# A gated-delta decode step: state products in two column halves, state updates in two row groups

## The chip, the core and the metric

The kernel runs on one core of one Trainium2 chip. The metric is device time in microseconds (us), the median over several executions. A profiled execution gives the trace.

## What is computed

One inference step of a one-layer hybrid decoder. A prompt of 2048 tokens and a group of 8 samples with 4 new tokens each go through the same weights: an adaptive layer norm, a wide input projection, a gated MLP branch and a gated DeltaNet branch with 8 heads, output projections and a last layer norm. All of it is in f32. The change lies in the DeltaNet branch, where each sample brings an old state per head:

```python
def step(S, xs):
    q_n, k_n, u_n, w_n, qk_n, gc_n = xs
    v_new = u_n - jnp.einsum('bhck,bhkv->bhcv', w_n, S)
    o = (jnp.einsum('bhck,bhkv->bhcv', q_n * jnp.exp(gc_n)[..., None], S)
         + jnp.einsum('bhcs,bhsv->bhcv', qk_n, v_new))
    g_last = gc_n[..., -1:]
    S = (S * jnp.exp(g_last)[..., None]
         + jnp.einsum('bhck,bhcv->bhkv', k_n * jnp.exp(g_last - gc_n)[..., None], v_new))
    return S, o
```

For the sample group this is one step for 8 samples of 4 tokens. A state `S` is 128x128, one for each sample and head.

## The kernel before

The prompt is worked in two halves of 1024 tokens; the 32 sample tokens ride along with the first half as 32 more columns. `main` (L953) walks a list of projections: for each weight column block of 128, every column group of the half (384, 384 and 256+32 tokens in the first half, 512 and 512 in the second) is a chain of 24 matmuls into one PSUM bank, operands split in a high and a low part (`project`, L906). These matmuls are the bulk of the kernel. In each half the first part of the list goes head by head: k, q, v and z of head h, then some gate columns. Beside it each head has its own streams: the token-major copies, the gram products, the inverse of a unit triangular matrix (`inverse`, L1412) and the recurrence over 8 chunks (`chain`, L1523). In the first half each head also has `sample_head` (L1631), the sample's recurrence, so it runs eight times.

All of these streams are Python generators. They yield an operation with an estimated duration, and the planner (`Sched.run`, L135) picks at each step the stream whose operation could start first by its model: each engine has a time at which it is free, and an operation may start `LAG` after what it depends on (L41: 400 ns for PE, 200 for ACT, DVE and POOL). Priorities break ties. The order in which the planner takes the operations is the order in which they are written to the engines' queues, and each engine works its queue in that order. Buffers are handed out by name (`_acquire`, L74). PSUM's 8 banks are `mm` (banks 0 to 2, projections), `po` (3 and 4, outputs of the chain) and `pt` (5 to 7, all else); `pu` is any of 3 to 7 (L294 to L297). `kx` is one buffer; `Rb` and `Xb` are two each, shared with the chain.

Operations are written by small helpers, so their trace lines are the helpers': L438 a matmul, L443 a transpose, L395 an ACT operation, L404, L414 and L420 DVE operations. Where a block yields once and then writes several matmuls itself, the line is its own: L641 (conditioning, four column quarters), L1470, L1476, L1479 (32x32 products of the inverse), L1496, L1507, L1509 (64x64 products).

In `sample_head` the steps that matter are these. k, q and v are made token-major (32 partitions), `kp` and `vs` are scaled rows of k and v, and `us` is the 32x32 inverse. `kx` holds, per sample, 64 columns: 32 for k and 32 for decayed q, nonzero only in that sample's four. Eight products (L1693 to L1695), one for each sample, 64 columns against the sample's 128x128 state, add up in one accumulation of 64 partitions: S^T k in partitions 0 to 31, S^T q in 32 to 63. DVE forms `vs` minus the first (L1698), ACT takes the second out (L1702). The product with `us` (L1705) gives the new v. It goes into the output product (L1709) and, after the states have been scaled by their decay (L1729), into the updates: twice, for four samples each, DVE spreads the new v over four column blocks with the selection constants `c_sel` (L1733), one product of 32 rows, 128 columns and 512 moving columns makes four updates (L1736), and DVE adds them to the states (L1739).

An f32 product is two records in the trace: two passes, each with its own weight load.

Of the kernel before, what the change touches and what calls it, by code (L numbers as in the profile page):

```python
# [11 lines left out]
ALU = mybir.AluOpType  # L12

P = 128
# [3 lines left out]
NB = 8  # L18
LS = 4
NS = NB * LS  # L20
# [149 lines left out]
def hybrid_step_kernel(ctx: ExitStack, tc: tile.TileContext, x_prompt, x_sample, state_conv, state_ssm,  # L170
# [4 lines left out]
    nc = tc.nc  # L175
# [39 lines left out]
    def V(off, *dims, p0=0, np_=P):  # L215
        dims = [[1, d] if isinstance(d, int) else list(d) for d in dims]
        t, o, st = place(off)
        return bass.AP(t.tensor, t.offset + p0 * st + o, [[st, np_]] + dims)

    def Q(bank, off, *dims, p0=0, np_=P):  # L220
        dims = [[1, d] if isinstance(d, int) else list(d) for d in dims]
        return bass.AP(PS.tensor, PS.offset + p0 * 4096 + bank * 512 + off, [[4096, np_]] + dims)
# [93 lines left out]
    S = Sched(98 + len(unit_names), roles)  # L316
# [13 lines left out]
    c_mns, c_sts, c_trb, c_sel = const(32), const(32), const(32), const(8)  # L330
# [3 lines left out]
    c_sbeta, c_sneg, c_sngc, c_kds = const(8), const(8), const(8), const(8)  # L334
# [46 lines left out]
    def act(out, in_, func=AF.Copy, dep=None, scale=None, bias=None, accum=None):  # L381
        ns = fsz(out) / 1.2 + (55 if in_ps(in_) else 95)
        ns += 93 * (not isinstance(scale, (int, float, type(None)))) + 93 * (bias is not None) + 150 * (accum is not None)
        if func in (AF.Ln, AF.Exp, AF.Tanh, AF.Gelu_apprx_tanh):
            ns += 1300 * ((func == AF.Ln) != S.ln_table)
            S.ln_table = func == AF.Ln
        t = yield ("o", "ACT", ns, dep)
        kw = {}
        if scale is not None:
            kw["scale"] = scale  # L390
        if bias is not None:
            kw["bias"] = bias
        if accum is not None:
            kw["accum_out"] = accum
        nc.scalar.activation(out, in_, func, **kw)  # L395
        return t
# [4 lines left out]
    def tt(out, a, b, op, dep=None, eng="DVE"):  # L401
        if eng == "DVE":
            t = yield ("o", "DVE", dve_ns(out, (a, b)), dep)
            nc.vector.tensor_tensor(out=out, in0=a, in1=b, op=op)  # L404
        else:
            t = yield ("o", "POOL", 240 + 2.15 * fsz(out), dep)
            nc.gpsimd.tensor_tensor(out=out, in0=a, in1=b, op=op)  # L407
        return t

    def ts(out, a, s1, op0, s2=None, op1=None, dep=None):  # L410
        aps = sum(not isinstance(s, (int, float, type(None))) for s in (s1, s2))
        t = yield ("o", "DVE", dve_ns(out, (a,), 1.0 if in_ps(a) else 2.0) + 60 * aps, dep)
        kw = dict(op1=op1) if op1 is not None else {}
        nc.vector.tensor_scalar(out=out, in0=a, scalar1=s1, scalar2=s2, op0=op0, **kw)  # L414
        return t

    def stt(out, a, s, b, op0, op1, dep=None):
        aps = not isinstance(s, (int, float))
        t = yield ("o", "DVE", dve_ns(out, (a, b)) + 60 * aps, dep)
        nc.vector.scalar_tensor_tensor(out=out, in0=a, scalar=s, in1=b, op0=op0, op1=op1)  # L420
        return t
# [14 lines left out]
    def mm(out, lhsT, rhs, start=True, stop=True, dep=None):  # L436
        t = yield ("o", "PE", pe_ns(lhsT, rhs), dep)
        nc.tensor.matmul(out, lhsT, rhs, start=start, stop=stop)  # L438
        return t
# [6 lines left out]
    def bc(ap, shape):  # L446
        return ap.to_broadcast(shape)
# [65 lines left out]
    def init_small():  # L513
        yield ("o", "DMA", 200.0, 0.0)
        nc.sync.dma_start(out=V(c_ong, 1), in_=DV(onorm_g, 0, [1, P], [1, 1]))
        nc.sync.dma_start(out=V(c_negA, 8), in_=DV(a_log, 0, [0, P], [1, 8]))
        nc.sync.dma_start(out=V(c_dtb, 8), in_=DV(dt_bias, 0, [0, P], [1, 8]))
        t = S.dma
        t = yield from act(V(c_negA, 8), V(c_negA, 8), AF.Exp, dep=t)
        t = yield from ts(V(c_negA, 8), V(c_negA, 8), -1.0, ALU.mult)  # L520
        t = yield from ts(V(c_ong, 1), V(c_ong, 1), 0.5, ALU.mult)
        S.signal("small", t)

    def init_vec():
        yield ("w", ("ada", 0))
# [1105 lines left out]
    def sample_head(h):  # L1631
        me = hd(0, h)
        t = 0.0
        for s in range(3):
# [24 lines left out]
        t = yield from ts(V(o_vf, 1, **k32), V(o_n, 1, **k32), 0.25, ALU.mult)  # L1659
        t = yield from pow_(V(o_vf, 1, **k32), V(o_vf, 1, **k32), 1)  # L1660
        kp, vs = x + 64, x + 192
        t = yield from ts(V(kp, P, **k32), Q(pb[0], 0, P, **k32), V(o_kf, 1, **k32), ALU.mult)
        t = yield from ts(V(vs, P, **k32), Q(pb[0], P, P, **k32), V(o_vf, 1, **k32), ALU.mult)
        S.release(pb, t)
        es, npq, am, m2, us = x + 320, x + 352, x + 416, x + 448, x + 480
        t1 = yield from tt(V(es, NS, **k32), V(gr, NS, **k32), V(c_mns, NS, **k32), ALU.add, dep=t1)
        t1 = yield from act(V(es, NS, **k32), V(es, NS, **k32), AF.Exp, bias=V(c_sngc + h, 1, **k32))
        egr = x + 32
# [4 lines left out]
                           bc(V(es, NS, **k32).unsqueeze(1), [NS, 2, NS]), ALU.mult, ALU.mult, dep=max(t, t1))  # L1673
        t = yield from tt(V(npq, NS, **k32), V(npq, NS, **k32), V(c_sts, NS, **k32), ALU.mult)
        t = yield from tp(Q(pb[0], 64, NS, **k32), V(npq, NS, **k32))
        t = yield from act(V(am, NS, **k32), Q(pb[0], 64, NS, **k32))
        t = yield from mm(Q(pb[0], 96, NS, **k32), V(am, NS, **k32), V(npq, NS, **k32))
        t = yield from tt(V(m2, NS, **k32), Q(pb[0], 96, NS, **k32), V(c_ident, NS, **k32), ALU.add)
        t = yield from mm(Q(pb[0], 128, NS, **k32), V(am, NS, **k32), V(m2, NS, **k32))
        t = yield from tt(V(us, NS, **k32), V(m2, NS, **k32), Q(pb[0], 128, NS, **k32), ALU.subtract)  # L1680
        S.release(pb, t)

        kb = yield ("a", "kx")
# [4 lines left out]
        nc.gpsimd.tensor_copy(V(kx, [68, 8], [1, 4]), V(sm, [4, 8], [1, 4]))  # L1688
        t3 = yield from tt(V(kx + 32, [68, 8], [1, 4]), V(sm + 32, [4, 8], [1, 4]), V(egr, [4, 8], [1, 4]),
                           ALU.mult, dep=max(t3, t2))  # L1690
        pb = yield ("a", "pt")
        t4 = 0.0
        for b in range(NB):  # L1693
            t4 = yield from mm(Q(pb[0], 0, P, np_=64), V(kx + 64 * b, 64), V(sb0[0] + b * P, P),
                               start=b == 0, stop=b == NB - 1, dep=max(t3, td, pb[2]))  # L1695
        S.release(kb, t4)
        rb = yield ("a", "Rb")
        t = yield from stt(V(rb[0], P, **k32), Q(pb[0], 0, P, **k32), V(c_sneg + h, 1, **k32), V(vs, P, **k32),  # L1698
                           ALU.mult, ALU.add, dep=max(t4, t, rb[2]))
        osb = yield ("a", "Xb")  # L1700
        q32 = dict(p0=32, np_=32)
        t5 = yield from act(V(osb[0], P, **q32), Q(pb[0], 0, P, **q32), dep=max(t4, osb[2]))  # L1702
        S.release(pb, max(t, t5))
        pb = yield ("a", "pt")
        t = yield from mm(Q(pb[0], 0, P, **k32), V(us, NS, **k32), V(rb[0], P, **k32), dep=max(t, pb[2]))  # L1705
        t = yield from act(V(rb[0], P, **k32), Q(pb[0], 0, P, **k32))
        tx = t

        t = yield from mm(Q(pb[0], P, P, np_=64), V(npq, 64, **k32), V(rb[0], P, **k32), dep=t)  # L1709
# [8 lines left out]
        t = yield from tp(Q(pb[0], 0, NS), V(osb[0], P, **q32), idn=V(c_ident + 32, NS, **q32), dep=max(t, pb[2]))  # L1718
        S.release(osb, t)
        tz = yield ("w", ("zz", 0, h, len(CG[0]) - 1))  # L1720
        ys = x + 448
        t = yield from stt(V(ys, NS), Q(pb[0], 0, NS), V(c_ong, 1), V(me["ZZ"][0] + HALF, NS),
                           ALU.mult, ALU.mult, dep=max(t, tz))
        S.release(pb, t)
# [3 lines left out]

        t2 = yield from tt(V(sb0[0], [P, 8], [1, P]), V(sb0[0], [P, 8], [1, P]),  # L1729
                           bc(V(egr + 3, [4, 8]).unsqueeze(2), [P, 8, P]), ALU.mult, dep=max(t2, t4))  # L1730
        for i in range(2):
            xe = yield ("a", "kx")
            t1 = yield from tt(V(xe[0], [P, 4], [1, P], **k32), bc(V(rb[0], P, **k32).unsqueeze(1), [NS, 4, P]),  # L1733
                               bc(V(c_sel + 4 * i, 4, **k32).unsqueeze(2), [NS, 4, P]), ALU.mult, dep=max(tx, xe[2]))
            pb = yield ("a", "pt")
            t = yield from mm(Q(pb[0], 0, 512), V(kp, P, **k32), V(xe[0], 512, **k32), dep=max(t1, pb[2]))  # L1736
            S.release(xe, t)
            a = V(sb0[0] + 512 * i, 512)
            t = yield from tt(a, a, Q(pb[0], 0, 512), ALU.add, dep=max(t, t2))  # L1739
            S.release(pb, t)  # L1740
        S.release(rb, t1)
        S.release(xb, max(t, S.ev[("smpdone", h)]))
        S.release(ss, t)
# [483 lines left out]
    def start():  # L2227
        S.spawn(x_take(0), 0.0)
        for i, j in enumerate((2, 0, 3, 1)):
            S.spawn(ada_block(j), 1.02 + 0.01 * i)  # L2230
        for c in range(9):
            S.spawn(x_norm(0, c, "xh0"), 1.0 + 0.001 * c)
        for cgi in range(3):
            S.spawn(x_done(cgi), 1.0)
            for k in range(KT):
                S.spawn(h_part(cgi, k), 1.5 + 0.1 * cgi + 0.01 * k)
# [16 lines left out]
    with tc.manual_schedule():  # L2253
        S.spawn(init_consts(), 0.0)
        S.spawn(init_ada(), 0.0)
        S.spawn(init_vec(), 1.015)
        start()
        S.spawn(init_small(), 1.02)
        S.spawn(wstream(groups), 1.0)
        S.spawn(main(), 9.0)  # L2260
        S.spawn(scal_free(), 5.0)
        S.spawn(conv_tail(), 3.0)
        S.spawn(v_take(), 1.0)
        S.spawn(inv_next(), 1.0)
        S.run()
# [37 lines left out]
```

## Time and profile before

| | us |
|---|---|
| median of 3 runs | 2743.01 |
| lowest, highest | 2738.87, 2744.91 |
| the profiled execution, its own time | 2741.66 |
| span of its instructions | 2739.8 |

In the profile PE is TensorE's matmuls and PEld its weight loads, DVE is VectorE, ACT ScalarE, POOL GpSimd. Matmuls are pipelined, and a record reaches from its start to the (modelled) end of its way through the array, so neighbouring records overlap. A form such as `128*64 128x128` is rows*columns of the array, then partitions x elements that move. In the timeline, neighbours of one line, operation and tiles stand in one row with their count: the row's length reaches from the first one's start to the last one's end.

### The profile page before, as it was taken

The numbers are of one execution on the slowest core, as the hardware profiler recorded it, in microseconds if no ns is written. First come the engines' busy times: TensorE is split into PE (matmuls) and PEld (weight loads), VectorE is DVE, ScalarE is ACT, GpSimd is POOL, SyncE is SP. The second block draws the span as 40 slices with busy tenths as digits, with TensorE's granted clock in tenths as the row PEclk, the third lists the DMA queues.
The fourth block names the chain that finished last, engine by engine and source line by source line (L and its number), as shares of the span: only waits on it lengthen the run. The fifth ranks groups of instructions, "written<-read, shape, count | busy, mean of one in ns | idle before, by whom it ended". The sixth has DMA issues, their size and how long they took to land. (4 is left out here: it accounts for less than half of the span.)

```text
span 2739.8 us, 43826 instructions
## 1 busy us (share of the span) xinstructions
PE 2692.0 (98%) x16514; PEld 2362.1 (86%) x16514; DVE 1445.9 (53%) x3194; ACT 1003.2 (37%) x2710; POOL 553.5 (20%) x1452
## 2 busy tenths in 40 slices
PE   6999999999999999999999999999999999999998
PEld 4989989998898999999997888788888888888876
DVE  5677666767552253433547655666663324433446
ACT  5544444545343322221224535444452312222120
POOL 2053444335300000000000443433341000000001
PEclk9999999999999999999999999999999999999999
DMA  6222332222553142233433222222223422233342
GB/s 213 59 70 70 84 90 63 74 69 62 152 190 95 58 125 77 86 111 92 138 109 102 79 77 69 69 61 66 77 59 92 123 95 80 71 114 104 104 124 84
DMA packets 360493, 255.88 MB, mean 93 GB/s; under 512 B 72793, under 2 KB 326033, under 8 KB 360282
## 3 DMA queue, kind: packets, MB, share of 16 engines
q1 hardware_dynamic: 360282, 253.10, 31.3%
q8 instruction: 129, 2.11, 0.3%
q14 instruction: 82, 0.67, 0.1%
HBM read 197.31 MB, written 55.71 MB: 92 GB/s over the span
## 5 line engine op out<-in xcount | busy, mean ns | idle before, releaser
L438 PE MATMUL psum<-TX,TWHL 128*128 128x384 f32 (+3 forms) x9296 | 1981.7, 361 | 3.8 <-DVE TX L404 3.4
L438 PEld LDWEIGHTS psum<-TX,TWHL 128*128 128x128 f32 (+1 forms) x9296 | 1551.8, 188 | 165.1 <-issue 10.8
L395 ACT ACTIVATE arena<-psum 128x128 bf16<-128x128 f32 (+8 forms) x920 | 311.8, 348 | 777.7 <-PE psum L438 620.8
L427 POOL TENSOR_TENSOR arena<-arena 128x1 f32<-128x1 f32 (+4 forms) x139 | 125.4, 903 | 1627.7 <-DVE arena L414 1412.2
L420 DVE SCALAR_TENSOR_TENSOR arena<-arena 128x512 f32<-128x512 f32 (+8 forms) x625 | 344.9, 561 | 92.3 <-ACT arena L395 81.0
L407 POOL TENSOR_TENSOR arena<-arena 128x60 f32<-128x60 f32 (+24 forms) x992 | 343.3, 346 | 132.7 <-DMA arena<-d_blk 26.7
L404 DVE TENSOR_TENSOR TWHL<-arena,TWHL 128x512 fp32r<-128x512 f32 (+1 forms) x344 | 235.4, 689 | 244.0 <-ACT TWHL L395 241.7
L420 DVE SCALAR_TENSOR_TENSOR arena<-arena,psum 128x128 f32<-128x128 f32 (+3 forms) x342 | 132.4, 403 | 361.2 <-PE psum L438 249.8
L395 ACT ACTIVATE TWHL<-arena 128x512 fp32r<-128x512 f32 x344 | 214.8, 627 | 206.8 <-PE psum L438 100.7
L395 ACT ACTIVATE arena<-arena 128x128 f32<-128x128 f32 (+8 forms) x509 | 228.3, 486 | 130.6 <-DVE arena L420 81.3
L443 PE MATMUL psum<-arena 128*128 128x128 f32 (+6 forms) x509 | 126.0, 271 | 2.5 <-ACT Y3F L395 0.8
L404 DVE TENSOR_TENSOR arena<-arena 128x3 f32<-128x3 f32 (+13 forms) x259 | 113.7, 447 | 18.6 <-DMA arena<-d_gc 8.7
L438 PE MATMUL psum<-arena 128*128 128x128 f32 (+6 forms) x524 | 101.6, 293 | 1.0 <-ACT arena L395 1.0
L420 DVE SCALAR_TENSOR_TENSOR arena<-psum,arena 128x512 f32<-128x512 f32 (+4 forms) x80 | 39.9, 510 | 109.8 <-PE psum L438 109.6
L1219 POOL COPY arena<-arena 128x3 f32<-128x3 f32 x120 | 35.8, 298 | 296.8 <-ACT arena L395 296.1
L438 PEld LDWEIGHTS psum<-arena 128*128 128x128 f32 (+5 forms) x524 | 73.8, 163 | 22.4 <-issue 12.7
L443 PEld LDWEIGHTS psum<-arena 128*128 128x128 f32 (+6 forms) x509 | 67.5, 137 | 26.4 <-issue 13.3
L395 ACT ACTIVATE Y7F<-psum 32x256 f32<-32x256 f32 (+6 forms) x115 | 46.6, 406 | 100.2 <-PE psum L438 39.0
L395 ACT ACTIVATE TX<-arena 128x512 fp32r<-128x512 f32 (+2 forms) x84 | 47.1, 586 | 93.1 <-DMA arena<-d_yb 75.7
L395 ACT ACTIVATION_READ_ACCUMULATOR arena<-psum 128x1 f32 (+1 forms) x392 | 76.6, 195 | 0.0
L414 DVE TENSOR_SCALAR arena<-arena 128x3 f32<-128x3 f32 (+10 forms) x234 | 47.6, 211 | 36.0 <-ACT arena L395 24.9
L404 DVE TENSOR_TENSOR TX<-arena,TX 128x512 fp32r<-128x512 f32 (+2 forms) x84 | 52.2, 638 | 24.8 <-ACT TX L395 24.4
(242 smaller groups left out, 2715.2 us busy)
## 6 DMA issues: line engine op xcount, KB each, us to landing
arena<-in_w_in_dram SPq DMA_DIRECT2D x288, 256.0 KB
out_dram<-arena SPq DMA_DIRECT2D x25, 512.0 KB
arena<-in_x_prompt_dram SPq DMA_DIRECT2D x24, 512.0 KB
arena<-d_gc SPq DMA_DIRECT2D x16, 512.0 KB
arena<-d_blk SPq DMA_DIRECT2D x64, 128.0 KB
d_yb<-arena SPq DMA_DIRECT2D x32, 256.0 KB
d_vh<-arena SPq DMA_DIRECT2D x16, 512.0 KB
arena<-d_vh SPq DMA_DIRECT2D x16, 512.0 KB
```

The costliest lines, as they stand in the source:

```text
L395: nc.scalar.activation(out, in_, func, **kw)
L404: nc.vector.tensor_tensor(out=out, in0=a, in1=b, op=op)
L407: nc.gpsimd.tensor_tensor(out=out, in0=a, in1=b, op=op)
L414: nc.vector.tensor_scalar(out=out, in0=a, scalar1=s1, scalar2=s2, op0=op0, **kw)
L420: nc.vector.scalar_tensor_tensor(out=out, in0=a, scalar=s, in1=b, op0=op0, op1=op1)
L427: nc.gpsimd.tensor_tensor(out=out, in0=a, in1=e, op=ALU.pow)
L438: nc.tensor.matmul(out, lhsT, rhs, start=start, stop=stop)
L443: nc.tensor.transpose(out, in_, ident[: in_.shape[0], : in_.shape[0]] if idn is None else idn)
L1219: nc.gpsimd.tensor_copy(V(c_tail + gi, [24, 3]), V(x0 + n0, 3))
```

## The change

In `sample_head` the eight state products are written as one block of the planner. Samples 0, 2, 4 and 6 accumulate in partitions 0 to 63 of the bank, samples 1, 3, 5 and 7 in partitions 64 to 127, so that they use the two column halves of the array. ACT then copies the upper half to SBUF, DVE adds the lower half, and the subtraction reads that sum. The inverse `us` is written twice side by side, so that the product with it puts the new v into partitions 0 to 31 and 32 to 63; `kp` is copied to partitions 32 to 63 as well, and so are four columns of the selection constants, once, at the start. One DVE operation over 64 partitions then spreads the new v for all eight samples, and the two update products are written as one block, one from partitions 0 to 31 and one from 32 to 63 (two row groups of the array), into two banks, the second from `pu`. Some scratch columns move to make room.

```diff
+    def init_sel():
+        t = yield ("w", ("ada", 0))
+        yield from ts(V(c_sel, 4, p0=32, np_=32), V(c_sel + 4, 4, np_=NS), 1.0, ALU.mult, dep=t)
...
         t = yield from ts(V(kp, P, **k32), Q(pb[0], 0, P, **k32), V(o_kf, 1, **k32), ALU.mult)
+        t = yield from ts(V(kp, P, p0=32, np_=32), V(kp, P, **k32), 1.0, ALU.mult, dep=t)
...
-        es, npq, am, m2, us = x + 320, x + 352, x + 416, x + 448, x + 480
+        es, npq, am, m2, us = x + 320, x + 352, x, x + 320, x + 416
...
-        t = yield from act(V(am, NS, **k32), Q(pb[0], 64, NS, **k32))
+        t = yield from act(V(am, NS, **k32), Q(pb[0], 64, NS, **k32), dep=max(t, t2))
...
-        t = yield from tt(V(us, NS, **k32), V(m2, NS, **k32), Q(pb[0], 128, NS, **k32), ALU.subtract)
+        t = yield from tt(V(us, [NS, 2], [1, NS], **k32), bc(V(m2, NS, **k32).unsqueeze(1), [NS, 2, NS]),
+                          bc(Q(pb[0], 128, NS, **k32).unsqueeze(1), [NS, 2, NS]), ALU.subtract)
...
-        t4 = 0.0
+        t4 = yield ("o", "PE", 4 * 230.0, max(t3, td, pb[2]))
         for b in range(NB):
-            t4 = yield from mm(Q(pb[0], 0, P, np_=64), V(kx + 64 * b, 64), V(sb0[0] + b * P, P),
-                               start=b == 0, stop=b == NB - 1, dep=max(t3, td, pb[2]))
+            nc.tensor.matmul(Q(pb[0], 0, P, p0=64 * (b % 2), np_=64), V(kx + 64 * b, 64), V(sb0[0] + b * P, P),
+                             start=b < 2, stop=b >= NB - 2)
         S.release(kb, t4)
-        rb = yield ("a", "Rb")
-        t = yield from stt(V(rb[0], P, **k32), Q(pb[0], 0, P, **k32), V(c_sneg + h, 1, **k32), V(vs, P, **k32),
-                           ALU.mult, ALU.add, dep=max(t4, t, rb[2]))
         osb = yield ("a", "Xb")
         q32 = dict(p0=32, np_=32)
-        t5 = yield from act(V(osb[0], P, **q32), Q(pb[0], 0, P, **q32), dep=max(t4, osb[2]))
-        S.release(pb, max(t, t5))
+        o64 = V(osb[0], P, np_=64)
+        t4 = yield from act(o64, Q(pb[0], 0, P, p0=64, np_=64), dep=max(t4, osb[2]))
+        t4 = yield from tt(o64, Q(pb[0], 0, P, np_=64), o64, ALU.add)
+        S.release(pb, t4)
+        t5 = t4
+        rb = yield ("a", "Rb")
+        t = yield from stt(V(rb[0], P, **k32), V(osb[0], P, **k32), V(c_sneg + h, 1, **k32), V(vs, P, **k32),
+                           ALU.mult, ALU.add, dep=max(t4, t, rb[2]))
         pb = yield ("a", "pt")
-        t = yield from mm(Q(pb[0], 0, P, **k32), V(us, NS, **k32), V(rb[0], P, **k32), dep=max(t, pb[2]))
-        t = yield from act(V(rb[0], P, **k32), Q(pb[0], 0, P, **k32))
+        t = yield from mm(Q(pb[0], 0, P, np_=64), V(us, 64, **k32), V(rb[0], P, **k32), dep=max(t, pb[2]))
+        t = yield from act(V(rb[0], P, np_=64), Q(pb[0], 0, P, np_=64))
...
-        for i in range(2):
-            xe = yield ("a", "kx")
-            t1 = yield from tt(V(xe[0], [P, 4], [1, P], **k32), bc(V(rb[0], P, **k32).unsqueeze(1), [NS, 4, P]),
-                               bc(V(c_sel + 4 * i, 4, **k32).unsqueeze(2), [NS, 4, P]), ALU.mult, dep=max(tx, xe[2]))
-            pb = yield ("a", "pt")
-            t = yield from mm(Q(pb[0], 0, 512), V(kp, P, **k32), V(xe[0], 512, **k32), dep=max(t1, pb[2]))
-            S.release(xe, t)
+        xe = yield ("a", "kx")
+        t1 = yield from tt(V(xe[0], [P, 4], [1, P], np_=64), bc(V(rb[0], P, np_=64).unsqueeze(1), [64, 4, P]),
+                           bc(V(c_sel, 4, np_=64).unsqueeze(2), [64, 4, P]), ALU.mult, dep=max(tx, xe[2]))
+        pb = yield ("a", "pt")
+        pc = yield ("a", "pu")
+        t = yield ("o", "PE", 900.0, max(t1, pb[2], pc[2]))
+        for i, q in enumerate((pb, pc)):
+            rows = dict(p0=32 * i, np_=32)
+            nc.tensor.matmul(Q(q[0], 0, 512), V(kp, P, **rows), V(xe[0], 512, **rows), start=True, stop=True)
+        S.release(xe, t)
+        te = t
+        for i, q in enumerate((pb, pc)):
             a = V(sb0[0] + 512 * i, 512)
-            t = yield from tt(a, a, Q(pb[0], 0, 512), ALU.add, dep=max(t, t2))
-            S.release(pb, t)
+            t = yield from tt(a, a, Q(q[0], 0, 512), ALU.add, dep=max(te, t2))
+            S.release(q, t)
```

## Rows read from the trace of the kernel before

**Rows 1.** Page, parts 1, 2: busy us (share of span); granted clock.

```profile
PE 2692.0 (98%) x16514; PEld 2362.1 (86%) x16514; DVE 1445.9 (53%) x3194; ACT 1003.2 (37%) x2710; POOL 553.5 (20%) x1452
PEclk9999999999999999999999999999999999999999
```

**Rows 2.** Table of waits, PE, 170 to 745 us: total us, times, longest.

```profile
PE psum L438 <- ACT arena L395: 0.7, 1, 0.7
PE psum L1507 <- ACT Y7F L395: 0.7, 1, 0.7
```

**Rows 3.** Groups by form, PE: rows*columns, moving; busy us, mean ns.

```profile
L438 PE MATMUL psum<-arena 128*64 128x128 f32 x128 | 16.3, 277 | 0.0
L438 PE MATMUL psum<-arena 32*128 32x512 f32 x32 | 17.9, 640 | 0.0
L438 PE MATMUL psum<-TX,TWHL 128*128 128x288 f32 x1920 | 305.0, 303 | 0.0
L1496 PE MATMUL psum<-arena,Y3F 64*64 64x64 f32 x128 | 5.9, 236 | 0.0
```

**Rows 4.** Timeline, PE, head 3's state products: start us, length us.

```profile
389.14 1.96 PE L438 MATMUL psum<-arena 128*64 128x128 f32 x16
391.03 0.53 PE L438 MATMUL psum<-TX,TWHL 128*128 128x288 f32 x2
```

**Rows 5.** Timeline, PE: 64x64 column halves; four column quarters.

```profile
415.67 0.68 PE L1496 MATMUL psum<-arena,Y3F 64*64 64x64 f32 x16
33.32 1.06 PE L641 MATMUL psum<-Y4F,Y7F 128*32 128x512 f32 x8
```

**Rows 6.** Timeline, PE, around head 3's first update.

```profile
403.12 0.56 PE L438 MATMUL psum<-TX,TWHL 128*128 128x288 f32 x3
403.61 1.12 PE L438 MATMUL psum<-arena 32*128 32x512 f32 x2
404.66 0.53 PE L438 MATMUL psum<-TX,TWHL 128*128 128x288 f32 x2
```

**Rows 7.** Timeline, PE, head 0's state products in pieces.

```profile
180.58 1.09 PE L438 MATMUL psum<-arena 128*64 128x128 f32 x8
181.60 0.33 PE L443 MATMUL psum<-arena 128*128 128x128 f32 x1
...
183.28 0.44 PE L438 MATMUL psum<-TX,TWHL 128*128 128x384 f32 x1
```

**Rows 8.** Timeline, PE, 32x32 products of the inverse.

```profile
411.39 0.69 PE L1470 MATMUL psum<-arena,Y3F 32*32 32x32 f32 x32
```

**Rows 9.** Timeline, DVE, ACT, PE behind head 3's state products.

```profile
391.14 0.34 DVE L420 SCALAR_TENSOR_TENSOR arena<-psum,arena 32x128 f32<-32x128 f32 x1 [4.86 <-PE psum L438]
391.52 0.27 ACT L395 ACTIVATE arena<-psum 32x128 f32<-32x128 f32 x1 [0.27 <-DVE arena L420]
392.29 0.40 PE L438 MATMUL psum<-arena 32*32 32x128 f32 x2
...
393.78 0.43 PE L438 MATMUL psum<-arena 32*64 32x128 f32 x2
```

**Rows 10.** Groups by form, DVE, 160 to 760 us.

```profile
L404 DVE TENSOR_TENSOR arena<-arena 32x512 f32<-32x512 f32 x16 | 10.8, 675 | 0.0
L414 DVE TENSOR_SCALAR arena<-arena 32x128 f32<-32x128 f32 x8 | 2.5, 316 | 3.5 <-POOL arena L427 3.4
L404 DVE TENSOR_TENSOR arena<-psum,arena 32x128 f32<-32x128 f32 x8 | 2.3, 284 | 11.9 <-PE psum L438 11.8
```

**Rows 11.** Windows: length, busy us (PE, PEld, DVE, ACT, POOL), clock, DMA.

```profile
400.00:490.00 90.00, 90.00 (x663) 82.24 (x661) 61.94 (x156) 43.14 (x146) 34.39 (x93) 1.00 0.27 72
750.00:755.00 5.00, 5.00 (x54) 4.02 (x44) 0.71 (x2) 1.72 (x5) 0.00 (x0) 0.66 0.27 92
```

**Rows 12.** Timeline, head 0's last reads of Y0, head 2's first write.

```profile
226.98 0.61 PE L438 MATMUL psum<-arena,Y0F 128*128 128x128 f32 x4
230.40 0.55 DVE L420 SCALAR_TENSOR_TENSOR Y0F<-arena 128x384 f32<-128x384 f32 x1
```

More of the change, by code (lines that the diff above doesn't have):

```diff
@@ L1720, in sample_head @@
         tz = yield ("w", ("zz", 0, h, len(CG[0]) - 1))
-        ys = x + 448
+        ys = x + 320
         t = yield from stt(V(ys, NS), Q(pb[0], 0, NS), V(c_ong, 1), V(me["ZZ"][0] + HALF, NS),
@@ L2256, in hybrid_step_kernel @@
         S.spawn(init_vec(), 1.015)
+        S.spawn(init_sel(), 1.6)
         start()
```

## The prediction

> **What bounds the kernel now.** I read the page first. TensorE (PE) is busy for 2692.0 us, 98% of the span, with nine tenths or more of the full clock granted in all 40 slices; no other engine passes 53% [rows 1]. An average can hide stages, so I looked next at the one stage that the change touches: the eight heads of the first half, from about 170 to 745 us, in which the sample's recurrence is threaded between the big projections. There the table of waits names two idle spells of PE, 0.7 us each, in 575 us [rows 2]. PE is the bound of this stage, and it is fed: what is taken off its queue should come off the time nearly whole. Work on VectorE (DVE), ScalarE (ACT) and POOL counts only if PE comes to wait for it.
>
> The groups by form then give the two kinds of PE work that are changed [rows 3]. The products with the states (128 rows, 64 columns, 128 moving columns) are 128 passes: 8 heads x 8 products, and each f32 product is two passes. The updates (32 rows, 128 columns, 512 moving columns) are 32 passes: 8 heads x 2 products x 2 passes.
>
> **Cost of the products with the states.** In head 3 (a row's second number reaches to the end of its last pass) the 16 passes start at 389.14 and the next projection pass starts at 391.03: 1.89 us [rows 4]. The row is 1.96 long and a pass lasts 0.28 [rows 3], so the last starts 1.68 after the first: 15 steps of 0.112. The change sends even samples to partitions 0-63 and odd ones to 64-127 of the same bank, so two chains of four products could run side by side. What does a step of such a pair cost? The nearest rows are in the inverse and at the start. L1496 runs 64x64 products in alternating column halves: 16 passes in 0.68 [rows 5], of which the last is 0.24 [rows 3], so 0.44 for the steps before it. With 64 columns, half of 128, one after the other they would need 15 steps of about 0.056, or 0.84; as 8 pairs it is 7 steps of 0.063. L641 uses all 128 rows and four column quarters with 512 moving columns: 8 passes in 1.06 [rows 5], where one update's 2 passes with as many moving columns take 1.12 [rows 6]. So column tiles do overlap, also with all rows in use. For 128 moving columns I add the 0.056 that 64 more cost a step: 0.063 + 0.056 = 0.119 a pair, 7 steps, 0.83 in place of 1.68. Saved: 0.85 us a head, 6.8 us for eight. The bounds are 0 (no overlap) and 8 steps fewer of 0.112, 0.90 a head; I take 0.85, since both rows overlap fully.
>
> The eight products are now handed to the planner as one block. Before, they could be split: head 0's stand in three pieces, from 180.58 to 183.28, 2.70 us with two foreign transposes between [rows 7]. Against 1.89 in one piece, and 0.11 for each transpose (a step of a 128-column pass, an estimate), a split costs (2.70 - 1.89 - 0.22) / 2 = 0.3. I count the two of head 0: 0.6 us.
>
> **Cost of the updates.** In head 3 the first update starts at 403.61 and the next projection pass at 404.66: 1.05 us [rows 6]. There is more at both edges. Three projection passes of 0.30 [rows 3] fill 0.56 before it, a step of 0.13, so the fourth was due at 403.51: 0.10 lost going in. The two behind it take 0.53 in place of 0.13 + 0.30: 0.10 lost coming out. One update costs 1.25 us, of which about 0.4 is edge and first weights. The change gives both updates one visit, the first from partitions 0-31, the second from 32-63, into two banks. If they overlap, a whole visit goes: 1.25 us a head, 10.0 us for eight. If the second pair of passes queues behind the first, it costs two more steps of 0.42 (L641's 1.06 [rows 5] less the 0.64 that a pass of 512 moving columns lasts [rows 3]) and the head saves 1.25 - 0.84 = 0.41. No row of before has two row groups feeding the same columns; the nearest are L1470's products, which differ in rows and columns and put 32 passes into 0.69 us [rows 8]. I take the full overlap, 1.25, as the row nearest in kind, and keep 0.41 for the range. It can't be worse than queueing, which is what happens now with edges on top.
>
> By the Trainium skill ("TensorE: Matmul & The Clock Gate", "Measured speedup vs the span model") four row tiles gave 3.07 times, not 4. Spread evenly that is some 10% on a pair's passes, by that page's figure an estimate of 0.7 us less gain over eight heads; the sum goes by the rows.
>
> **What is added.** The product with the inverse takes 64 columns in place of 32; the two forms lie side by side as 0.40 and 0.43 [rows 9], so +0.03 a head, 0.2 us. On DVE the second 32x512 selection product (0.68) goes; a copy of k to partitions 32-63 (0.32) and the sum of the two halves (0.28) come [rows 10]; the one selection left has 64 partitions and as many elements in each. That is nothing net, and DVE is busy 62 of 90 us in a head's stretch [rows 11]. ACT's evacuation only changes partitions. The selection constants' copy at the start is one small operation. No DMA is added or moved, so no queue of SP's changes.
>
> One new wait matters. The state products were read by the subtraction on DVE and by ACT at once; now ACT copies the upper half, DVE adds the lower, and only then comes the subtraction, and the product on PE waits for it. In head 3 the subtraction ended at 391.48 and the product started at 392.29, with projection passes between: 0.8 us of cover. The two new steps are 0.27 and 0.28 long [rows 9, 10]. They fit, and the planner, which counts them and a lag on each, will put the product later; there are projections to put before it. If the cover were gone, each us would be a us of PE. The second bank (from 3 to 7, shared with the chain's outputs) is held until the adds end; the tightest place I see for a delayed chain is head 0's, which stops reading Y0 at 227.6 while head 2 writes it at 230.40 [rows 12]: 2.8 us of cover.
>
> **Sum.** 6.8 + 0.6 + 10.0 - 0.2 = 17.2 us. The profiled execution took 2741.66, which gives 2724.5; it lies 1.35 below the median of 2743.01. I forecast 2725.
>
> **Rivals.** (A) Row groups that share columns do not overlap: updates save 0.41 a head, 3.3 in all, so 6.8 + 0.6 + 3.3 - 0.2 = 10.5, 2731. For it: no row shows such a pair. Against: every tiled pair in the trace overlaps.
> (A2) The two passes of a product stay together and the second product's first pass starts only beside the first one's second: three steps in place of two, 0.42 a head less, 3.4 us, 2728; the column chains would lose one step of eight. L641 speaks against it: so staggered, its 8 passes would take five steps of 0.42 and not the 1.06 seen [rows 5]. The Trainium skill, same page, "The mechanism", states that matmuls start strictly in program order, which would give this if the program has a product's two passes side by side.
> (B) The change does not do what it says: nothing overlaps, only the edges go: 0.6 + 3.3 - 0.2 = 3.7, about 2738.
> (C) The gain is real but the planner's new order makes PE wait elsewhere and gives 5 to 12 us back: 2730 to 2737. For it: the order of every engine is laid out again. Against: the stage has 1.4 us of waits now.
> (D) Slower: the product behind the three-step evacuation stands at the head of PE's queue and is not ready. Price: 1 us of PE for each us that ACT and DVE run late beyond the cover, in each of eight heads. It decides from 17.2 / 8 = 2.2 us a head; at 3 us, 24 us are lost: 2748 or 2749. Against: the two steps together are 0.55 us and the longest DVE operation beside them would have to come in between each time.
>
> **How the numbers follow.** Forecast 0.68, A 0.09, A2 0.04, B 0.05, C 0.08, D 0.06. The range 2719 to 2737 holds forecast, A, A2 and most of C. It also takes in one more thing: at 750 to 755 us the granted clock is 0.66 of full on average [rows 11], that is, part of this stretch ran at 1.2 GHz in place of 2.4; whether a shifted timetable repeats that is worth up to 2 us either way. About 0.2%, 5.5 us, is what can be told from no change: faster (under 2737.5) has the forecast, A, A2 and most of C, 0.86; same has B and the rest of C, 0.08; slower 0.06.
>
> **What would show it.** In the profile after: each head's 16 state passes in one row of about 1.1 us in place of 1.96; one row of four update passes a head, about 1.1 us if they overlap, 1.6 under A2, 2.0 under A; PE's waits from 170 to 730 us still a few us in sum; head 7's last update some 15 us earlier, and everything behind shifted by as much. I am wrong if the four update passes take 2 us, or if PE's idle spells before the inverse's product grow to 1 us or more a head.

## The result, and the profile after

The changed kernel takes 2724.97 us (median of 6 runs, 2721.58 to 2729.7) against 2741.97 before: a ratio of 0.9938, 95% interval 0.9926 to 0.9949. That is 17.0 us, and 2725 was forecast. A second set on another occasion gave 2722.5 against 2741.4 (0.9926, 0.9913 to 0.9939). The profiled execution took 2726.29 us, with a span of 2724.4.

The page of the changed kernel (called after below), parts 1 and 2, beside [rows 1]: PE is still busy for 98% of its span, but for 14 us less; DVE and ACT have not moved by more than 2 us. The one 8 in the row of the granted clock is a slice that is taken up below.

```profile
PE 2678.3 (98%) x16514; PEld 2357.7 (87%) x16514; DVE 1447.5 (53%) x3203; ACT 1001.7 (37%) x2710; POOL 551.0 (20%) x1452
PEclk9999999999999999999999999899999999999999
```

The groups by form (busy us, mean ns), beside [rows 3]. There are as many passes as before, each as long as before, but the union of their times is half as much: this is what overlap looks like in such a row.

```profile
L1752 PE MATMUL psum<-arena 32*128 32x512 f32 x32 | 9.0, 640 | 0.0
L1703 PE MATMUL psum<-arena 128*64 128x128 f32 x128 | 8.8, 279 | 0.0
```

PE's timeline in head 3 of after, first the state products (beside [rows 4]), then the updates (beside [rows 6]). The 16 state passes fill 1.09 us and not 1.96; the four update passes of a head fill 1.13, hardly more than the two of a single update did (1.12), and the second visit (PE's going over from the projections to an update and back) is gone.

```profile
377.28 0.69 PE L438 MATMUL psum<-TX,TWHL 128*128 128x384 f32 x3
377.90 1.09 PE L1703 MATMUL psum<-arena 128*64 128x128 f32 x16
378.92 0.44 PE L438 MATMUL psum<-TX,TWHL 128*128 128x384 f32 x1
...
394.08 0.69 PE L438 MATMUL psum<-TX,TWHL 128*128 128x384 f32 x3
394.70 1.13 PE L1752 MATMUL psum<-arena 32*128 32x512 f32 x4
395.75 0.62 PE L438 MATMUL psum<-TX,TWHL 128*128 128x384 f32 x2
```

PE's waits of after, from 165 to 732 us (beside [rows 2]): one, at the very end, in head 7's inverse. None stands at the product behind the three-step evacuation.

```profile
PE psum L1500 <- DVE arena L414: 1.9, 1, 1.9
```

[rows 2] end at 745 us, ahead of the same place of the kernel before. Up to 752 us that kernel has two more waits, in head 7's inverse too, so its sum is 3.0 and not 1.4:

```profile
PE psum L1476 <- ACT Y7F L395: 1.1, 1, 1.1
PE psum L1479 <- DVE Y7F L414: 0.5, 1, 0.5
```

Where in the time the gain arises can be read off the projections, since their passes come in the same order in every kernel (counted are the passes of L438 that read TX or TWHL and move 288 columns or more). Starts of the same projection pass, in us from the span's start (the last column is the second profile of the changed kernel, from the control run below):

```
pass     before    after   control
  400     130.5    131.3     132.5
 3000     762.6    744.8     746.4
 7000    1481.5   1461.5    1462.7
 7700    1693.4   1672.0    1674.7
 8000    1785.4   1768.9    1765.9
11000    2585.8   2569.8    2566.8
```

From pass 400 to 3000, the eight heads, after gains 18.6 us; by pass 7700 it has 22.2. Then it loses 4.9 within 100 us, and the control does not. The page of windows (length; busy us of PE, PEld, DVE, ACT, POOL; granted clock; DMA) for the same 15 us of after and, below it, of the control:

```profile
1705.00:1720.00 15.00, 12.90 (x131) 9.45 (x132) 9.92 (x19) 5.04 (x17) 3.12 (x4) 0.57 0.01 1
```

```profile
1705.00:1720.00 15.00, 13.15 (x158) 9.70 (x157) 12.69 (x24) 7.00 (x19) 3.24 (x4) 1.00 0.10 23
```

In after the clock stands at 1.2 GHz for most of this stretch, and 131 passes are recorded in it and not 158. Ahead of it PE had waited for the third inverse of the second half, in both executions, 2.14 us in after and 1.32 in the control (idle time in brackets; after first):

```profile
1707.10 1.07 PE L1474 MATMUL psum<-arena,Y2F 32*32 32x32 f32 x32 [2.14 <-DVE arena L1450]
```

```profile
1708.87 0.69 PE L1474 MATMUL psum<-arena,Y2F 32*32 32x32 f32 x32 [1.32 <-DVE arena L1450]
```

It is the same program. So this loss belongs to one execution and not to the change.

### The profile page after: what moved, and what is told of

It is laid out like the page before. It is cut to its first block, busy times and chain, and to the rows that moved or that the text cites. A ratio compares the mean times of both kernels' runs of the same rounds, so it can differ in the third digit from the quotient of the medians.

```text
span 2724.4 us, 43839 instructions
## 1 busy us (share of the span) xinstructions
PE 2678.3 (98%) x16514; PEld 2357.7 (87%) x16514; DVE 1447.5 (53%) x3203; ACT 1001.7 (37%) x2710; POOL 551.0 (20%) x1452
## 5 line engine op out<-in xcount | busy, mean ns | idle before, releaser
L438 PE MATMUL psum<-TX,TWHL 128*128 128x384 f32 (+3 forms) x9296 | 1984.7, 361 | 3.8 <-DVE TX L404 3.4
L438 PEld LDWEIGHTS psum<-TX,TWHL 128*128 128x128 f32 (+1 forms) x9296 | 1555.4, 189 | 162.1 <-issue 7.0
L427 POOL TENSOR_TENSOR arena<-arena 128x4 f32<-128x4 f32 (+4 forms) x139 | 122.4, 881 | 1620.8 <-DVE arena L414 1420.6
L420 DVE SCALAR_TENSOR_TENSOR arena<-arena 128x512 f32<-128x512 f32 (+9 forms) x633 | 348.1, 559 | 93.4 <-ACT arena L395 83.6
L443 PE MATMUL psum<-arena 128*128 128x128 f32 (+7 forms) x509 | 125.6, 270 | 3.2 <-ACT TX L395 1.0
L404 DVE TENSOR_TENSOR arena<-arena 128x3 f32<-128x3 f32 (+12 forms) x251 | 108.1, 438 | 17.8 <-DMA arena<-d_gc 6.7
L443 PEld LDWEIGHTS psum<-arena 128*128 128x128 f32 (+7 forms) x509 | 67.5, 137 | 25.5 <-issue 11.6
L395 ACT ACTIVATION_READ_ACCUMULATOR arena<-psum 128x1 f32 x392 | 76.6, 195 | 0.0
L438 PEld LDWEIGHTS psum<-arena 128*128 128x128 f32 (+3 forms) x364 | 55.9, 171 | 18.1 <-issue 8.5
L414 DVE TENSOR_SCALAR arena<-arena 128x3 f32<-128x3 f32 (+8 forms) x243 | 50.4, 214 | 36.3 <-ACT arena L395 27.6
L438 PE MATMUL psum<-arena 128*128 128x128 f32 (+4 forms) x364 | 67.5, 269 | 1.1 <-ACT arena L395 1.0
```

Of the source, the lines that this page charges most:

```text
L427: nc.gpsimd.tensor_tensor(out=out, in0=a, in1=e, op=ALU.pow)
L443: nc.tensor.transpose(out, in_, ident[: in_.shape[0], : in_.shape[0]] if idn is None else idn)
```

## The experiments

Two theories stood against each other. The first is the forecast's: PE bounds the eight heads, and each part is worth the passes and edges that it takes off PE's queue, because tiled passes overlap. The second: the gain comes from something else that the change brings along, one visit of PE in place of two, eight products in one block, or simply a luckier order of the planner. Times below are medians. The runs were made in two sets. In the first, differences are given against the control, the changed kernel itself; the second (the order in twos, each part alone, two holds) has no control and is compared with the kernel before. Edits are shown against the changed kernel; dots stand for lines left out.

**The control.**

> The changed kernel once more, as the control for the others of this set. Both theories: 17 us under the kernel before, about 2725 us. If the stretch at 1.2 GHz around 1707 to 1721 us of its first profile is a matter of chance it may be absent here, and the time is then about 2720; if it belongs to the wait ahead of the third inverse of the second half, it is there again.

Measured: 2722.51 us (2717.69 to 2723.48). The stretch at 1.2 GHz is absent in its profile, and the time is near the 2720 that was named for that case.

**Both updates from one row group.** This isolates the overlap of the row groups: order, planner's costs and visits stay.

```diff
-            rows = dict(p0=32 * i, np_=32)
+            rows = dict(p0=0, np_=32)
```

> Both update products take their operands from partitions 0 to 31, so the second has the same row group as the first; order, planner's costs and all other work are as in the changed kernel (the second four samples' states get the first four's update, which is not what the reference computes). Theory 1 (the row groups overlap, which is worth two passes a head): the four passes of a head take 0.43 us each one behind the other, 0.85 us more a head, 6.8 us in all: 2732. Theory 2 (the gain of the updates came from the one visit in place of two, not from overlap): no slower than the changed kernel, 2725.

Measured: 2729.77 us, 7.3 over the control (0.9956 of before, 0.9943 to 0.997; control 0.9926). In head 3 of its timeline the four passes now stand behind each other:

```profile
397.94 1.98 PE L1752 MATMUL psum<-arena 32*128 32x512 f32 x4
```

1.98 in place of 1.13 us is 0.85 a head, 6.8 for eight, as expected; from pass 400 to 3000 this profile is 6.5 us longer than the control's (620.4 against 613.9). So the overlap of these two row groups, which feed the same columns, is real and full; the rest of the updates' gain is the visit saved. This also shows what rival A would have looked like.

**The order of the eight state products.**

```diff
-        for b in range(NB):
+        for b in (0, 2, 4, 6, 1, 3, 5, 7):
```

> The eight state products are written in the order of samples 0, 2, 4, 6, 1, 3, 5, 7, so four of one column half stand in front of four of the other; everything else is as in the changed kernel, the output too. Theory 1 (products start in program order, and overlap because neighbours lie in different halves): the halves run one behind the other, each head's block takes about 1.7 us to its last start in place of 0.82, 0.87 us more a head, 7 us in all: 2732. Theory 2 (each half works its own line of products): no change, 2725.

Measured: 2730.56 us (2723.89 to 2731.55), 8.0 over the control; but its profiled execution, at 2723.89 the fastest of its six, is 0.4 over the control's (of which it had gained 2.2 ahead of the heads: its pass 400 starts at 130.3, the control's at 132.5). The profile says why neither theory holds. Head 3's block:

```profile
378.31 1.58 PE L1703 MATMUL psum<-arena 128*64 128x128 f32 x16
```

1.58 lies between 1.09 (alternating) and 1.96 (one half only, [rows 4]): 0.49 us a head lost, 3.9 in all, not 7 and not 0. (From pass 400 to 3000 this profile is 3.5 us longer than the control's, 617.4 against 613.9.) The single records don't name their half; it is read from their starts. The first half's passes start 0.11 us apart (the second of them 0.16 behind the first); the second half's first pass starts 0.006 us behind the fifth of them, at 378.800, while the first half's sixth, seventh and eighth start after it, from 378.903 on. So a product of the other half may start ahead of earlier ones, but here only three passes ahead. Whatever half a record belongs to, the block's last start comes 1.31 us after its first, and not the 1.7 that was expected of the program's order. The median's other 4 us against the control I cannot place: no profile of a slower execution of this kernel exists, though the granted clock of those runs is lower (0.992 and 0.993 against 0.996 in the profiled one).

**The order in twos.**

```diff
-        for b in range(NB):
+        for b in (0, 2, 1, 3, 4, 6, 5, 7):
```

> The eight state products in the order of samples 0, 2, 1, 3, 4, 6, 5, 7; all else as in the changed kernel. With four and four (the run e4_order) the second half's first pass started beside the fifth of the first half's eight, so 3 passes that stood in front of it had not started. Theory 1 (a half's product may start up to four passes ahead of the program's order): with two and two, four passes, the halves overlap nearly from the start; from the first to the last start of a head's block about 0.82 to 0.95 us, as in the changed kernel. Theory 2 (strictly in the program's order): sample 1's first pass can't start before sample 2's second one; counting it through gives about 1.37 us.

Measured, in one execution of 2727.48 us, is the block of head 3:

```profile
382.18 1.14 PE L1703 MATMUL psum<-arena 128*64 128x128 f32 x16
```

Less a pass of 0.28 that is 0.86 to the last start, as theory 1 has it, and not 1.37. With two and two the order costs 0.05 us; with four and four 0.49.

**Each part alone.** For the columns alone, the updates, the product with the inverse and the selection are those of before; for the rows alone, the state products and their evacuations are.

The first, and below it the second, cut to the PE part:

```diff
-        t = yield ("o", "PE", 900.0, max(t1, pb[2], pc[2]))
-        for i, q in enumerate((pb, pc)):
-            rows = dict(p0=32 * i, np_=32)
-            nc.tensor.matmul(Q(q[0], 0, 512), V(kp, P, **rows), V(xe[0], 512, **rows), start=True, stop=True)
+        for i in range(2):
...
+            t = yield from mm(Q(pb[0], 0, 512), V(kp, P, **k32), V(xe[0], 512, **k32), dep=max(t1, pb[2]))
```

```diff
-        t4 = yield ("o", "PE", 4 * 230.0, max(t3, td, pb[2]))
         for b in range(NB):
-            nc.tensor.matmul(Q(pb[0], 0, P, p0=64 * (b % 2), np_=64), V(kx + 64 * b, 64), V(sb0[0] + b * P, P),
-                             start=b < 2, stop=b >= NB - 2)
+            t4 = yield from mm(Q(pb[0], 0, P, np_=64), V(kx + 64 * b, 64), V(sb0[0] + b * P, P),
+                               start=b == 0, stop=b == NB - 1, dep=max(t3, td, pb[2]))
```

> The state products as in the changed kernel (one block, two column halves), the updates, the inverse and the selection as in the kernel before. Theory 1 (each part is worth what its passes and edges cost on PE): 6.8 for the halves and 0.6 to 0.9 for the splits that are gone, so 7.5 us under the kernel before, about 2734. Theory 2 (the gain is the planner's new order and not the parts): either about no gain or about the whole 19 us. In the profile 16 state passes a head in about 1.1 us, update passes two and two as before.

> The updates, the inverse and the selection as in the changed kernel (two row groups, one visit), the state products as in the kernel before. Theory 1: 9.8 us for one visit less a head, less 0.2 for the wider product with the inverse, so 9.6 us under the kernel before, about 2732. Theory 2: about no gain or about the whole 19 us. The two parts should add up to the whole within 3 us.

Measured: columns alone 2730.23 against 2744.42 before (0.9953, 0.9942 to 0.9965: 12.9 us, 10 to 16); rows alone 2733.45 (0.9961, 0.9948 to 0.9973: 10.7 us, 7 to 14). By these times the rows came out as expected and the columns brought 5 us more, and the two add up to 24, not to the 17 or 19 of the whole in the two other sets. To see where, I cut the stretch from pass 400 to pass 3000 by what PE did in it, from the starts of its records (us; a part's time runs from its first start to the next instruction's; "way in" is what the pass ahead of it takes beyond its columns; waits are taken out of the other rows; remainders of missing records are left out):

```
                        before  after  columns  rows
state products           15.56   8.19     8.20  16.00
way into them             1.53   0.84     0.83   1.95
updates                  16.82   8.46    16.82   8.46
way into them             1.86   0.97     1.90   0.84
products behind them      5.51   5.73     5.51   5.72
the inverse              20.50  20.26    19.82  20.84
waits                     3.49   2.28     0.00   4.69
whole stretch           632.08 613.51   619.20 625.86
```

The parts themselves are additive: the columns take 8.06 off the state products in both kernels that have them, the rows 9.25 to 9.38 off the updates. So are the whole stretches: 12.9 us for the columns and 6.2 for the rows are 19.1, and the changed kernel has 18.6. But neither kernel gets just its part. With the columns alone PE has no wait left (3.5 us before) and the inverse is 0.7 us shorter; with the rows alone the waits grow by 1.2 us, and the planner cut the state products of four heads into pieces, which costs 0.9. I put both down to the planner's order, which every edit lays out anew; no run changes that order alone. Beside the parts they come to about 5 us for the columns and 3 against the rows. So that the rows' median came out as expected is luck: 6.2 us arise in the eight heads, another 2.1 behind them in the profiled execution, and the rest is what executions differ by. Theory 1 stands for the parts; a luckier or unluckier order comes on top.

**Holding the planner back.** PE waits at two places that follow from the planner's model being too early: the third inverse of the second half, and the 64x64 products of head 7's inverse in the first half. The first kernel has a hold at the one, the second at both.

```diff
-        t = yield ("o", "PE", 16 * 38.0 + 120, max(t, pb[2], pc[2], Zb[2]))
+        hold = 3000.0 if (half, h) == (1, 2) else 0.0
+        t = yield ("o", "PE", 16 * 38.0 + 120, max(t, pb[2], pc[2], Zb[2]) + hold)
```

The second kernel has this as well:

```diff
-        t = yield ("o", "PE", 16 * 32.0 + 140, max(ta, pb[2]))
+        late = 2500.0 if (half, h) == (0, 7) else 0.0
+        t = yield ("o", "PE", 16 * 32.0 + 140, max(ta, pb[2]) + late)
```

> The changed kernel, but the planner takes the first products of the third inverse of the second half for ready 3 us later than its model says, so that more projection passes go in front of them. Theory 1 (the clock fell to 1.2 GHz because PE waited 2.1 us there, and that gave back about 5 us): no wait, no stretch at 1.2 GHz around 1707 to 1721 us, 5 us under the control: 2720. Theory 2 (the clock falls there anyway): within 1 us of the control.

> The changed kernel with the planner's hold of 3 us on the third inverse of the second half (as in e5_hold) and one of 2.5 us on the 64x64 products of head 7's inverse in the first half, where PE waits 1.9 to 2.2 us. Theory 1 (a wait of PE that projection passes can fill is worth its length): 2 us under e5_hold, about 2718. Theory 2 (the planner moves the wait elsewhere): as e5_hold, about 2720. If the clock no longer falls to 1.2 GHz behind 730 us, another 1.7 us go.

Measured: one hold 2720.22 us (0.9923, 0.991 to 0.9936), two holds 2723.5 (0.9928, 0.9916 to 0.9941), the control 0.9926. None can be told from the changed kernel. In the profile the wait ahead of the third inverse is gone, but one of 1.2 us stands a few steps later in the same inverse (waits of PE from 1690 to 1740 us, one hold):

```profile
PE psum L1484 <- DVE Y7F L414: 1.2, 1, 1.2
```

So the first hold mostly moved the wait. With two holds the wait at head 7's 64x64 products is gone too and one of 1.0 us takes its place. The stretch at 1.2 GHz that after and the control have behind head 7's inverse is absent there, but the 1.7 us named for it don't show in the median, and that profile spends 24 us at 1.2 GHz at the start.

Whether the clock's fall at 1707 us needs the wait is not settled, but the wait's length alone does not decide it. Of the ten profiles of this case, four show 1.2 GHz at this inverse: after for 13.6 us with a wait of 2.1; one row group and the columns alone for 3.4 us each, with waits of 2.3 and 1.4; two holds for 6.8 us, with a wait of 1.5 some steps later. Six don't: five had waits of 0.9 to 1.4 us there, the control among them, and the sixth, the order in twos, had the longest of all, 2.6. The one profile of the kernel before is among the six, which is too little to say whether the new order makes such falls likelier.

## Why the prediction was right, point by point

**PE is the bound.** Right. What left PE's queue left the time: 18.6 us from pass 400 to 3000, of which 8.06 + 9.25 - 0.22 = 17.1 are the parts of the forecast as the table has them; 1.2 are waits that are gone and 0.4 the inverse's products with the way into them. The forecast's sum was 17.2. Not in the table is the way out, what the first pass behind a part takes beyond its columns: about 1 us less in after. The other passes of the stretch take as much more, and where they do is open.

**State products.** Forecast 6.8 for the halves and 0.6 for two splits. Measured 8.06 with the way in; a block's last start went from 1.69 to 0.82 us, 0.87 a head, where 0.85 was taken from the 64x64 products. The rest is splits and edges: before, the records show three splits and not two, two in head 0 and one in head 7, whose blocks reach their last start 0.81 and 0.40 us later than the other six. Less 0.11 for each foreign transpose that is 0.9 us, the 0.3 a split of the forecast.

**Updates.** Forecast 1.25 a head, 10.0; measured 9.25. The mechanism was right, and so is the size: the forecast's 1.25 counts the way out, 0.10, which the table leaves out. The first pass behind a visit takes about 0.10 us beyond its columns in every kernel, in sum 1.7 us behind the 16 visits of before and 0.8 behind the 8 of after. With these 0.8 us the updates gave 10.1. Sharing the array cost the pair next to nothing: its four passes fill 1.13 us, one update's two filled 1.12. Rival A is refuted by the run with one row group, A2 by the timeline: a head's two first passes start 0.007 us apart.

**The added wait.** The cover was read right. In head 3 of after the sum of the halves starts at 379.69 and the subtraction at 380.01, and PE's product follows at 381.45 (DVE, then PE). The subtraction took 0.50 here (0.33 to 0.34 in the seven other heads), which leaves 0.9 us of cover; over the eight heads it is 0.7 to 2.1. Rival D's waits did not come.

```profile
379.69 0.28 DVE L404 TENSOR_TENSOR arena<-psum,arena 64x128 f32<-64x128 f32 x1
380.01 0.50 DVE L420 SCALAR_TENSOR_TENSOR arena<-arena 32x128 f32<-32x128 f32 x1
...
381.45 0.43 PE L438 MATMUL psum<-arena 32*64 32x128 f32 x2
```

DVE is busy for 61.46 of 88 us in a head's stretch, against 61.94 of 90 [rows 11]: nothing net, as forecast.

**What was not in the sum.** Beyond the heads after gained another 3.6 us by pass 7700 and lost 4.9 with the clock. That the forecast fell within 0.1 us of the median is partly luck: the control's set gave 18.9 us. The clock's part was named as worth up to 2 us, from the stretch behind head 7's inverse, which did come again (0.83 of full from 725 to 735 us). It is absent in the two profiles in which PE waits least there, not at all (columns alone) or for 1.0 us (two holds); in the eight others PE waits 1.6 us or more. The larger one, at 1707, was not foreseen.

```profile
725.00:735.00 10.00, 8.11 (x108) 6.87 (x107) 3.24 (x7) 4.10 (x10) 0.00 (x0) 0.83 0.37 106
```

## What to carry to other kernels

Where PE is the bound and is fed, as here, small products in the wrong shape cost their full passes, and two of them in different column halves, or in different row groups with two banks, cost hardly more than one. Write them alternately: here PE started a pass at most three passes ahead of its turn. Count the way into and out of a tiled stretch as well (here about 0.4 us an update visit with the first weights), as merging two visits is worth that even without overlap. And where a planner lays the whole order out anew, expect a few us of luck in either direction, and look for the parts in the stretch they belong to, not in the total.

## What the runs showed of the hardware

Passes for the other column half can start out of the program's order: with the order four and four, three passes of one half that stood earlier started after the first of the other half. Strictly in order, the block in twos would have needed about 1.37 us to its last start, by the count made ahead of its run, and took 0.86 to 0.87. The Trainium skill ("TensorE: Matmul & The Clock Gate", "The mechanism") has matmuls start strictly in order; for these tiles the measurement decides against it. In the run four and four the second half's first pass started with three earlier ones not yet started, and not when there were four; whether this is PE's reach in general was not tried.

Executions of one program differ by several us, in part with the granted clock. Of 11 executions of the kernel before in the first set, the one with a mean of 0.998 took 2737.35 us and the three at 0.993 took 2742.52, 2745.55 and 2746.96; in the second set the link is looser (2741.82 to 2746.28 at 0.994, 2745.61 at 0.995). A spread of nearly 10 us is more than half of what this change is worth, so a part's price is better read from the trace of its stretch than from a single time.
